# Index scores over all 128 contraction rows, and half of layer 0's modulation moved beside them

## The chip, the cores and the metric

The kernel runs on one core of a Trainium2 chip. The metric is the device time of one execution in microseconds (us). Five engines work side by side, each with its own instruction stream: TensorE (PE; its weight loads are listed as PEld), VectorE (DVE), ScalarE (ACT), GpSimd (POOL) and SyncE (SP, whose queue issues the DMAs). They wait for one another by semaphores. The profile was taken of one execution on the chip; L12 is line 12 of the kernel.

## The reference, cut to what matters

The program is a two-layer encoder trunk over 1024 positions of width 1024. Each sub-layer is modulated by a vector that comes from a conditioning row c:

```python
cond = jax.nn.silu(c)
mod = (cond @ ada_w[l] + ada_b[l])[:, None, :]
sh_m, sc_m, g_m, sh_f, sc_f, g_f = jnp.split(mod, 6, axis=-1)     # parts 0 to 5
h = x * (1.0 + sc_m) + sh_m
y = even_mixer(h, ...)                                            # layer 0
x = layer_norm(DN_ALPHA * x + (1.0 + g_m) * y, ...)
h = x * (1.0 + sc_f) + sh_f
y = conv_ffn(h, ...)
x = layer_norm(DN_ALPHA * x + (1.0 + g_f) * y, ...)
```

Layer 0's mixer is a sparse attention beside a short gated convolution. One projection `z = h @ w_in` gives q, k, v, the index queries `q_idx` (8 heads of 64), one index key `k_idx` of 64, the weights of the index heads and the three inputs of the convolution. For each block of 128 queries an index score picks the 256 keys that the attention may see:

```python
rel = relu(einsum('bthd,bsd->bths', q_idx, k_idx))
score = einsum('bths,bth->bts', rel, w_idx)
_, idx = lax.top_k(where(admissible, score, NEG), 256)
```

Parts 0 and 1 of the modulation are needed before the projection. Parts 2 to 5 of layer 0 are needed later: part 2 when the mixer's output projection is added to the residual, parts 3 and 4 in the norm behind it, part 5 in the feed-forward net.

## The kernel before, in words

**Precision.** A float32 product is made of three matmuls of a 32-bit format with fewer mantissa bits (fp32r): each operand is split into a high part (ACT casts it) and a low part (DVE or POOL subtracts), and high times high, high times low and low times high are summed in PSUM. `mm3` (L288 to L290) is this triple; a projection of 512 positions is 8 of them, thus 24 matmuls over 128 rows and 512 columns.

**Index queries and keys.** The index head has only 64 dimensions, so the kernel stacks: for each head, `stack` (to L1299) puts the high part of the query into 64 rows of the tile `qi[:, head]` and the low part into the other 64. Even heads have the high part in rows 0 to 63, odd heads in rows 64 to 127. The key's high part `kih` and low part `kil` stand twice each, in both halves of the rows.

**Scores.** `index` (L1528) goes over query blocks i from 7 down to 2, and inside over four heads; it is called twice, for heads 0 to 3 and 4 to 7. For each head `scores2` makes a score tile of 128 queries by (i+1)*128 keys in a PSUM tile `idx_s` (two buffers), in pieces of 512 keys or fewer. Each piece is a pair of matmuls: L1307 takes all 128 rows of `qi` with `kih` (high and low query times high key), L1308 only the 64 rows with the high part with `kil`. ACT applies relu into `rl` (two buffers, L1537); DVE adds it, times the head's weight, to the block's score `dd[i]` (L1540, L1542). Behind each head `index` takes 1.4 (first call) or 1.6 (second call) steps from a generator of projections, each one `mm3`; these are what PE does between scores.

**Search.** The 256th largest score of each row is found by a bit search over 31 bits. Per bit, DVE proposes a candidate (L1618), ACT counts by signs in three blocks (L1624), DVE counts in the other three (L1576), then DVE decides (L1636, L1637). In this stage the order of DVE and ACT is the written one. Each bit also takes `mods.step()`, and nine of ten advance the projections by one product of 512 positions. When a product is finished, its result is copied out and, for each second one, the next weight is split (L266 on ACT, L267 on DVE). Behind the bits come an exact step, the counts and the masks (L1642 to L1672), and then the attention.

**Modulation.** `Modulation` holds a list of (part, block) pairs. A step loads a 128x1024 block of `ada_w` (512 KB) and multiplies it by the row silu(c), summing along the row, in one DVE instruction (L377). Behind the eighth block of a part the bias is added (L340, L342). Before the change the 32 steps of parts 2 to 5 are all in the search; their blocks go into the buffers `eq` and `pre` in turn, and silu(c) stands in a PSUM tile `cond_row`.

**What sets the order.** PE runs in the order in which the program is written. In the index stage the order of the other engines comes from a planner; its costs and priorities are not touched here. SP issues the DMAs of one queue in order.

Of the kernel before, what the change touches and what calls it, by code (L numbers as in the profile page):

```python
# [20 lines left out]
D = 1024  # L21
# [185 lines left out]
def trunk(ctx, tc, t, out):  # L207
    nc = tc.nc
    V, A, G, T = nc.vector, nc.scalar, nc.gpsimd, nc.tensor

    def pool(name, bufs=1, side="left", space=None):
        if space is not None:
            return tc.tile_pool(name=name, bufs=bufs, space=space, reuse_waits="tile")
        return tc.tile_pool(name=name, bufs=bufs, side=side, reuse_waits="tile")
# [12 lines left out]
    def spend(us):  # L227
        clock[0] += us
# [21 lines left out]
    def bank(name):  # L250
        return mm.tile([P, HALF], F32, tag="mm", name=name)
# [3 lines left out]
    def bank2(name):  # L255
        return aux[0].tile([P, S], F32, tag="s", name=name)
# [4 lines left out]
    def half(hf):  # L261
        return slice(hf * HALF, (hf + 1) * HALF)

    def split(hi, lo, src, lo_eng="dve"):

        A.copy(hi, src)  # L266
        (V if lo_eng == "dve" else G).tensor_tensor(lo, src, hi.bitcast(F32), ALU.subtract)  # L267
# [1030 lines left out]
            A.copy(dst[n][own, c], src[own])  # L1298
            V.tensor_tensor(dst[n][rest, c], src[own], dst[n][own, c].bitcast(F32), ALU.subtract)  # L1299

    def scores2(ps, i, q, kh, kl, rows):

        qc = slice(i * P, (i + 1) * P)
        w = (i + 1) * P
        for c in range(0, w, HALF):
            e = min(c + HALF, w)
            T.matmul(ps[:, c:e], lhsT=q[:, qc], rhs=kh[:, c:e], start=True, stop=False)  # L1307
            T.matmul(ps[:, c:e], lhsT=q[rows, qc], rhs=kl[rows, c:e], start=False, stop=True)  # L1308
            spend(2 * max(e - c, 256) / 2400.0)


# [16 lines left out]
    start = ExitStack()  # L1328
    tmp0 = start.enter_context(pool("start", bufs=3))
    bias0 = bias_of(0, tmp0)  # L1330
    kih = ip.tile([P, S], F32R, name="kih")
    kil = ip.tile([P, S], F32R, name="kil")
    wiT = ip.tile([P, S], F32, name="wiT")
    wi = ip.tile([P, 8, 8], F32, name="wi")
    qi = ip.tile([P, 8, S], F32R, name="qi")
# [67 lines left out]
    for hf in range(2):  # L1403
        c = half(hf)
        ps = first[0][2][:, c]
# [10 lines left out]
    def more_queries(m, w=None):  # L1416

        halves = range(2) if w is None else range(1, 2)
        w = w or weights(t["w_ev"][m], f"qi{m}")
        for hf in halves:  # L1420
            ps = bank("qi")
            for k, x in enumerate(h.xs(hf)):
                o = slice(k * P, (k + 1) * P)
                mm3(ps, (w[0][:, o], w[1][:, o]), x, k == 0, k == KD - 1)
                if k == KD - 1:
                    stack((qi[:, 2 * m], qi[:, 2 * m + 1]), ps, half(hf))
                yield
# [4 lines left out]
    ps = bank("wit")  # L1432
# [11 lines left out]
    class Projections:  # L1444
# [75 lines left out]
        def taps(self, m):  # L1520
            u, y = self.conv["u"], yb[:, m]
            A.mul(y, u[:, 0:S], ctap[:, m, 0:1])
            for k in (1, 2):
                V.scalar_tensor_tensor(
                    y, u[:, k : k + S], ctap[:, m, k : k + 1], y, ALU.mult, ALU.add
                )

    def index(heads, others, rate):  # L1528
        n = 0.0
        for i in range(7, 1, -1):  # L1530
            w_ = (i + 1) * P
            for hd in heads:
                rows = slice(64 * (hd % 2), 64 * (hd % 2) + 64)
                ps = bank2("idx_s")
                scores2(ps, i, qi[:, hd], kih, kil, rows)
                rl = tmp.tile([P, S], F32, tag="rl", name="rl")
                A.activation(rl[:, :w_], ps[:, :w_], AF.Relu)  # L1537
                wc = wi[:, i, hd : hd + 1]
                if hd == 0:
                    V.tensor_scalar(dd[i], rl[:, :w_], wc, None, ALU.mult)  # L1540
                else:
                    V.scalar_tensor_tensor(dd[i], rl[:, :w_], wc, dd[i], ALU.mult, ALU.add)  # L1542
                n += rate
                while n >= 1.0:
                    next(others, None)
                    n -= 1.0
    products = Projections().steps()
    index(range(4), chain(more_queries(3), products), FILL[0])
    index(range(4, 8), products, FILL[1])
    ipx.close()  # L1550
    yb = evy.enter_context(pool("evyb")).tile([P, 4, S], F32, name="yb")
    evkv = ExitStack()
# [14 lines left out]
    tk = sel.enter_context(pool("tk", side="right"))  # L1567
    eq = tk.tile([P, S], F32, name="eq")
    pre = tk.tile([P, S], F32, name="pre")
    junk = [tk.tile([P, S], BF16, name=f"junk{e}") for e in "va"]  # L1570

    cond_row = bank2("cond_row")
    mods = Modulation(None, tk, 0, range(2, 6), D, 0, cond_row, (eq, pre))

    def count(cnt, d, w, thr, op):
        V.tensor_scalar(junk[0][:, :w], d, thr, 0.0, op, ALU.add, accum_out=cnt)  # L1576
# [99 lines left out]
    def advance():  # L1676
        while next(products, True) is False:
            pass
# [3 lines left out]
    with tc.manual_schedule(engines={E.DVE}):  # L1682
        rows_ = Rows()
        rows_.setup()
        with tc.manual_schedule(engines={E.Activation}):
            pace = 0.0
            for bit in range(30, -1, -1):
                rows_.propose(bit)
                rows_.signs()
                rows_.counts()  # L1690
                mods.step()
                pace += PACE
                if pace >= 1.0:
                    advance()
                    pace -= 1.0
                rows_.decide()
            advance()
            mods.step()
        for nm, src in (("q", q32), ("k", k32)):
            split(*pairs[0, nm], src[:, 0])  # L1700
        rows_.step_up()
        rows_.result()
        rows_.mask()
# [147 lines left out]
    with ExitStack() as s:  # L1851
# [35 lines left out]
        for hf in range(2):  # L1887
            c = half(hf)
            xs = h.xs(hf)
            for base, n, mi, lo in ((4, 3, 0, 0), (7, 2, 1, 3)):  # L1890
# [18 lines left out]
                for m in range(n):  # L1909
                    ps = blocks[m][0]  # L1910
# [14 lines left out]
            for m in (3, 0, 1, 2) if hf else range(4):  # L1925
                w = weights(t["w_od"][m], f"u{hf}_{m}", lo_eng="pool")
                ps = bank("u")
# [33 lines left out]
    with ExitStack() as s:  # L1961
# [97 lines left out]
        for j in range(8):  # L2059
            ps = bank("uv")  # L2060
# [63 lines left out]
def build(nc, arrays):  # L2124
    t = {
        k: nc.dram_tensor(f"in_{k}", v.shape, mybir.dt.from_np(v.dtype), kind="ExternalInput").ap()
        for k, v in arrays.items()
    }
    out = nc.dram_tensor("out_xT", (KD, P, S), F32, kind="ExternalOutput").ap()
    with tile.TileContext(nc, schedule_with_timeline_sim=True) as tc:  # L2130
        trunk(tc, t, out)
# [15 lines left out]
```

## Time and profile before

| | us |
|---|---|
| median of the 3 runs shown (lowest, highest) | 2689.89 (2680.07, 2691.18) |
| the profiled execution | 2674.74 |
| its span, first to last instruction | 2672.9 |

| engine | busy us | share of the span |
|---|---|---|
| PE | 2467.4 | 92% |
| PEld | 1936.7 | 72% |
| DVE | 2157.8 | 81% |
| ACT | 1364.8 | 51% |
| POOL | 1054.5 | 39% |

The table is read as an average over stages with different limits. Matmuls are pipelined and their ends are modelled: in the timeline one bar reaches into the next, and the distance from start to start is what a matmul costs. The mean granted clock of TensorE is 0.969 of full speed; the low level is 0.50 in this unit.

### The profile page before, as it was taken

What the parts mean: (1) busy time and instruction counts of PE and PEld (TensorE: products, weight loads), DVE (VectorE), ACT (ScalarE), POOL (GpSimd) and SP (SyncE); (2) the same over time, 40 slices, a digit from 0 to 9 for tenths busy, and PEclk for the clock granted to TensorE, in tenths of its full rate; (3) what the DMA queues carried; (4) which work ended last, traced back from release to release, by engine and by line L of the source; (5) the groups of instructions that cost most, each with busy time, mean ns of one, the idle gap of its engine ahead of it and who ended that gap; (6) DMA issues with size and microseconds to landing.
All of it is one profiled execution on the core that took longest, in us unless ns stands there. A gap on an engine that the chain in (4) does not pass through costs nothing. (4 is left out here: it accounts for less than half of the span.)

```text
span 2672.9 us, 32638 instructions
## 1 busy us (share of the span) xinstructions
PE 2467.4 (92%) x10922; PEld 1936.7 (72%) x10922; DVE 2157.8 (81%) x3491; ACT 1364.8 (51%) x2427; POOL 1054.5 (39%) x800
## 2 busy tenths in 40 slices
PE   6999998999888989998999899999888999998997
PEld 5567776887666767786777677787666888877786
DVE  6549899777698999978887866877698877788977
ACT  3446751765554444554333546766464555563434
POOL 0000001645674222424547634643865333334546
PEclk9899999999989989999999999999989999999999
DMA  6004430013434555335323331123533322244313
GB/s 244 32 18 136 139 118 16 17 68 120 129 104 153 183 173 166 126 98 178 91 75 95 105 101 61 54 75 106 173 100 103 107 86 84 95 128 148 102 47 105
DMA packets 123690, 284.43 MB, mean 106 GB/s; under 512 B 15361, under 2 KB 23042, under 8 KB 122626
## 3 DMA queue, kind: packets, MB, share of 16 engines
q1 hardware_dynamic: 122370, 278.16, 32.8%
q10 hardware_dynamic: 1152, 4.19, 0.4%
q8 instruction: 86, 1.41, 0.2%
q14 instruction: 82, 0.67, 0.1%
HBM read 234.06 MB, written 48.23 MB: 106 GB/s over the span
## 5 line engine op out<-in xcount | busy, mean ns | idle before, releaser
L702 DVE SCALAR_TENSOR_TENSOR cv<-u,taps,cv 128x512 f32<-128x512 f32 x352 | 311.1, 910 | 19.1 <-ACT cv L700 17.5
L267 POOL TENSOR_TENSOR v<-v,v 128x512 fp32r<-128x512 f32 x8 | 12.6, 1580 | 443.6 <-ACT v L266 443.6
L998 DVE SCALAR_TENSOR_TENSOR r<-dn,mod,r 128x512 f32<-128x512 f32 x198 | 147.0, 745 | 44.4 <-PE dn L290 42.5
L833 POOL TENSOR_TENSOR s<-rawg 128x512 f32<-128x512 f32 (+3 forms) x60 | 79.4, 1323 | 256.4 <-DVE wlo_ups L267 87.3
L700 ACT ACTIVATE cv<-u,taps 128x512 f32<-128x512 f32 x176 | 124.3, 721 | 58.0 <-DMA z<-cv 32.8
L288 PE MATMUL up<-t,wh 128*128 128x512 f32 x288 | 119.5, 415 | 33.1 <-ACT u L872 33.1
L706 ACT ACTIVATE cv<-cv 128x512 f32<-128x512 f32 x88 | 55.6, 632 | 144.7 <-DVE cv L702 143.9
L289 PE MATMUL up<-h_f,whi_up 128*128 128x512 f32 x256 | 105.5, 412 | 24.8 <-DVE h_f L267 24.8
L872 ACT COPY u<-up 128x512 f32<-128x512 f32 x144 | 83.9, 583 | 75.8 <-issue 35.3
L267 DVE TENSOR_TENSOR wl<-rawg,wh 128x512 fp32r<-128x512 f32 (+3 forms) x120 | 116.1, 970 | 2.6 <-ACT wh L266 2.4
L289 PE MATMUL up<-t,wh 128*128 128x512 f32 x288 | 117.7, 409 | 0.0
L290 PE MATMUL up<-t,wl 128*128 128x512 f32 x288 | 117.3, 407 | 0.0
L288 PE MATMUL up<-h_f,whi_upa 128*128 128x512 f32 x288 | 114.6, 398 | 1.2 <-ACT whi_upa L266 1.2
L834 POOL TENSOR_TENSOR s<-s,raw_upv 128x512 f32<-128x512 f32 x36 | 51.4, 1428 | 161.9 <-DMA raw_upv<-in_w_up 145.7
L266 ACT CAST wh<-rawg 128x512 fp32r<-128x512 f32 (+3 forms) x120 | 65.0, 545 | 97.6 <-PE dn L289 52.4
L290 PE MATMUL up<-h_f,wlo_upa 128*128 128x512 f32 x288 | 113.7, 395 | 0.7 <-DVE wlo_upa L267 0.7
L267 DVE TENSOR_TENSOR pl<-pt,ph 128x128 fp32r<-128x128 f32 (+2 forms) x192 | 99.4, 546 | 18.3 <-ACT ph L266 18.1
L266 ACT CAST ph<-pt 128x128 fp32r<-128x128 f32 (+2 forms) x192 | 85.3, 480 | 54.6 <-PE pt L1197 53.1
L289 PE MATMUL up<-h_f,whi_upa 128*128 128x512 f32 x288 | 113.0, 392 | 0.0
L290 PE MATMUL up<-h_f,wlo_up 128*128 128x512 f32 x256 | 104.6, 409 | 6.0 <-POOL wlo_up L267 6.0
L288 PE MATMUL up<-h_f,whi_up 128*128 128x512 f32 x256 | 106.4, 416 | 2.9 <-ACT h_f L266 1.9
L1624 ACT ACTIVATE junka<-dd,cand 128x384 bf16<-128x384 f32 (+2 forms) x93 | 87.1, 936 | 39.9 <-DVE cand L1618 37.9
(750 smaller groups left out, 8617.3 us busy)
## 6 DMA issues: line engine op xcount, KB each, us to landing
mod_raw<-in_ada_w SPq DMA_DIRECT2D x96, 256.0 KB, 2.9
z<-cv SPq DMA_DIRECT2D x88, 256.0 KB, 2.0
raw_upv<-in_w_up SPq DMA_DIRECT2D x36, 512.0 KB, 3.7
rawg<-in_w_up SPq DMA_DIRECT2D x34, 512.0 KB, 3.7
raw_up<-in_w_up SPq DMA_DIRECT2D x32, 512.0 KB, 3.7
z<-z SPq DMA_DIRECT2D x56, 256.0 KB, 2.9
xa_dram<-xo SPq DMA_DIRECT2D x48, 256.0 KB, 2.1
raw_dr<-in_w_dr SPq DMA_DIRECT2D x32, 384.0 KB, 3.1
```

Source lines behind the costliest of these rows:

```text
L266: A.copy(hi, src)
L267: (V if lo_eng == "dve" else G).tensor_tensor(lo, src, hi.bitcast(F32), ALU.subtract)
L288: T.matmul(ps, lhsT=wh, rhs=xh, start=start, stop=False, skip_group_check=more)
L289: T.matmul(ps, lhsT=wh, rhs=xl, start=False, stop=False, skip_group_check=more)
L290: T.matmul(ps, lhsT=wl, rhs=xh, start=False, stop=stop, skip_group_check=more)
L700: A.activation(y[n], u[:, 0:HALF], AF.Copy, scale=self.taps[:, c, 0:1])
L702: V.scalar_tensor_tensor(y[n], u[:, k : k + HALF], self.taps[:, c, k : k + 1], y[n], ALU.mult, ALU.add,)
L706: A.activation(y[1], y[1], AF.Silu)
L833: G.tensor_tensor(s1, g[:, c0], g[:, c1], ALU.add)
L872: A.copy(dst, ps)
L998: V.scalar_tensor_tensor(r, ps, self.gate[:, dt : dt + 1], r, ALU.mult, ALU.add)
L1624: A.activation(junk[1][:, :w], d, AF.Sign, bias=self.col(self.cand.bitcast(F32), j), scale=-1.0, accum_out=self.col(self.cnt, j),)
```

## The change

Three edits. `scores2` no longer takes the 64 rows of its second matmul: L1308's instruction covers all 128 rows of `qi` and `kil`, so that low query times low key is summed too. A modulation object for parts 2 and 3 is made before the index scores, with a pool of its own (three load buffers of 512 KB in all partitions, a row of c, a bias), and steps once behind each even head of the blocks 7 to 3, up to its 16 steps: ten in the first call of `index`, six in the second. The search keeps parts 4 and 5: 16 steps, at odd bits and once behind the loop.

```diff
-    def scores2(ps, i, q, kh, kl, rows):
+    def scores2(ps, i, q, kh, kl):
...
             T.matmul(ps[:, c:e], lhsT=q[:, qc], rhs=kh[:, c:e], start=True, stop=False)
-            T.matmul(ps[:, c:e], lhsT=q[rows, qc], rhs=kl[rows, c:e], start=False, stop=True)
+            T.matmul(ps[:, c:e], lhsT=q[:, qc], rhs=kl[:, c:e], start=False, stop=True)
...
+    modx = ExitStack()
+    modp = modx.enter_context(pool("modp"))
+    mods = Modulation(modp, modp, 0, range(2, 4), D, 3)
+
     def index(heads, others, rate):
...
             for hd in heads:
-                rows = slice(64 * (hd % 2), 64 * (hd % 2) + 64)
                 ps = bank2("idx_s")
-                scores2(ps, i, qi[:, hd], kih, kil, rows)
+                scores2(ps, i, qi[:, hd], kih, kil)
+                if i > 2 and hd % 2 == 0:
+                    mods.step()
...
     index(range(4, 8), products, FILL[1])
+    modx.close()
     ipx.close()
...
-    mods = Modulation(None, tk, 0, range(2, 6), D, 0, cond_row, (eq, pre))
+    mods = Modulation(None, tk, 0, range(4, 6), D, 0, cond_row, (eq, pre))
...
                 rows_.counts()
-                mods.step()
+                if bit % 2:
+                    mods.step()
```

## Rows read from the trace of the kernel before

**Rows 1.** The page, part 1: busy us, share of the span, instructions of each engine.
```profile
PE 2467.4 (92%) x10922; PEld 1936.7 (72%) x10922; DVE 2157.8 (81%) x3491; ACT 1364.8 (51%) x2427; POOL 1054.5 (39%) x800
```

**Rows 2.** Windows, index stage: us; busy (instructions) PE, PEld, DVE, ACT, POOL; PEclk, DMA, GB/s.
```profile
82.60:96.40 13.80, 13.80 (x26) 7.23 (x26) 3.74 (x5) 3.07 (x3) 0.00 (x0) 0.50 0.00 0
96.40:199.00 102.60, 102.60 (x345) 60.84 (x345) 45.71 (x51) 41.91 (x58) 0.00 (x0) 1.00 0.05 16
```

**Rows 3.** Waits from 83 to 199 us: total us, times, longest.
```profile
ACT rl L1537 <- PE idx_s L1308: 69.6, 46, 3.6
```

**Rows 4.** Timeline of PE, one score pair between projections: start, duration, instruction.
```profile
128.63 0.39 PE L1307 MATMUL idx_s<-kih,qi 128*128 128x512 f32 x1
128.95 0.49 PE L1308 MATMUL idx_s<-kil,qi 64*128 64x512 f32 x1
129.37 0.50 PE L288 MATMUL q<-h_m,whi_q 128*128 128x512 f32 x1
129.70 0.40 PE L289 MATMUL q<-h_m,whi_q 128*128 128x512 f32 x1
129.94 0.39 PE L290 MATMUL q<-h_m,wlo_q 128*128 128x512 f32 x1
```

**Rows 5.** Timeline of PE, first attention scores behind the last projection.
```profile
448.50 0.39 PE L290 MATMUL bg<-h_m,wlo_('bg', 3)_2958 128*128 128x512 f32 x1
448.82 0.44 PE L288 MATMUL s<-kh,qh 64*128 64x384 f32 x1
449.10 0.34 PE L289 MATMUL s<-kl,qh 64*128 64x384 f32 x1
449.28 0.34 PE L290 MATMUL s<-kh,ql 64*128 64x384 f32 x1
```

**Rows 6.** Windows of the search and of the wait before the attention.
```profile
211.00:376.00 165.00, 156.75 (x672) 124.92 (x671) 149.12 (x360) 121.04 (x224) 0.00 (x0) 0.98 0.45 134
...
450.00:460.00 10.00, 0.83 (x5) 0.47 (x3) 9.86 (x11) 0.00 (x0) 0.00 (x0) 0.74 0.00 0
```

**Rows 7.** Timeline of DVE in the search: two bits (of 31), from proposal to proposal.
```profile
231.81 0.17 DVE L1618 TENSOR_TENSOR cand<-small,bits 128x6 int32<-128x6 int32 x1
...
236.20 0.17 DVE L1618 TENSOR_TENSOR cand<-small,bits 128x6 int32<-128x6 int32 x1
...
239.06 1.22 DVE L377 CUSTOM_DVE_ANT_0 eq<-eq,cond_row 128x1024 f32<-128x1024 f32 x1
240.20 0.08 DVE L377 DVE_READ_ACCUMULATOR2_ANT mod_acc<- 128x1 f32 x1
240.59 1.23 DVE L267 TENSOR_TENSOR wlo_('k', 3)_1590<-raw_('k', 3)_1513,whi_('k', 3)_1589 128x1024 fp32r<-128x1024 f32 x1 [0.32 <-ACT whi_('k', 3)_1589 L266]
...
242.14 0.17 DVE L1618 TENSOR_TENSOR cand<-small,bits 128x6 int32<-128x6 int32 x1
```

**Rows 8.** The tile idx_s: count, ns min/median/max, first and last start, forms.
```profile
L1308 PE MATMUL idx_s<-kil,qi x80: 323/491/793, 83.4 to 198.3; 64*128 64x512 f32 x48, 64*128 64x384 f32 x16, 64*128 64x256 f32 x8, 64*128 64x128 f32 x8
```

**Rows 9.** Timeline of PE in the stretch at the low clock.
```profile
89.00 0.79 PE L1308 MATMUL idx_s<-kil,qi 64*128 64x512 f32 x1
89.72 0.79 PE L288 MATMUL qi<-h_m,whi_qi 128*128 128x512 f32 x1
90.32 0.63 PE L289 MATMUL qi<-h_m,whi_qi 128*128 128x512 f32 x1
```

**Rows 10.** Timeline of ACT in the second of those bits.
```profile
239.43 0.19 ACT L1624 ACTIVATION_READ_ACCUMULATOR junka<-dd,cand 128x1 f32 x1
239.52 1.04 ACT L266 CAST whi_('k', 3)_1589<-raw_('k', 3)_1513 128x1024 fp32r<-128x1024 f32 x1
```

**Rows 11.** DMA issues: count, KB each, median us from issue to landing.
```profile
pre<-in_ada_w SPq DMA_DIRECT2D x16, 512.0 KB, 3.7
```

**Rows 12.** Timeline of PE and PEld among projections.
```profile
429.37 0.39 PE L289 MATMUL xb<-h_m,whi_('xb', 3)_2898 128*128 128x512 f32 x1
429.37 0.19 PEld L290 LDWEIGHTS xb<-h_m,wlo_('xb', 3)_2899 128*128 128x128 f32 x1
```

## The prediction

> **What bounds the kernel now.** I read the page first: TensorE (PE) is busy for 92% of the span, ahead of every other engine [rows 1]. That share is an average, so I looked up the two stages that the change touches by their windows. The index scores run from 82.6 to 199 us. PE is busy for all of these 116 us, first at the lower clock level (granted 0.50, 13.8 us), then at the full one; VectorE (DVE) is busy for 3.7 + 45.7 = 49.5 us and ScalarE (ACT) for 45 us, and DMA is nearly idle [rows 2]. The waits of that stretch say the same: ACT's relu waited 69.6 us for the score matmuls, in 46 waits [rows 3]. So the index stage is bound by PE.
>
> Next is what PE does in it. In the timeline a busy bar overlaps the next one, so the distance between starts is what counts. Full-height matmuls of 512 columns follow each other in 0.233 us (129.70 to 129.94 is one such step, rounded). Around a score pair it is slower [rows 4]: from the 128-row matmul to the 64-row one 0.32, from that to the next 0.42, and the projection behind the pair still takes 0.33. Each change between a 128-row and a 64-row matmul costs something on both of its sides. The attention shows that the change does it, and not the smaller height: there the first 64-row matmul starts 0.32 behind the 128-row one before it, the next (384 columns) 0.28 on, and from then on 64-row matmuls follow in 0.18 [rows 5].
>
> The search (31 bits, 211 to 376 us and the last one) is another case: PE is busy 156.8 of 165 us and DVE 149.1 [rows 6]. DVE's timeline gives 4.39 us for a bit with the modulation's multiply-and-sum, and 5.94 us for the next, in which a projection weight is split too [rows 7]; the two kinds alternate over most of the 31 bits. Behind the search DVE finishes the masks alone: from 450 to 460 us it is busy 9.9 us and PE 0.8 [rows 6].
>
> **The change, part by part.**
>
> Score matmuls. No instruction is added: the second matmul of each pair has the same columns and reads 128 rows where it read 64. What goes is the change of height. The three steps of the pair in [rows 4] take 0.32 + 0.42 + 0.33 = 1.07 us; dense they would take 3 x 0.233 = 0.70. That is 0.37 a pair, and there are 80 pairs [rows 8]. (Pairs with a narrower second piece differ by a few hundredths either way.) In the 13.8 us at the lower level PE gets through 26 matmuls [rows 2], 6 pairs among them. A pair costs more there: 0.72 from the 64-row matmul to the next and 0.60 behind that [rows 9], and 0.72 taken for the step inside the pair too, against 0.47 each (twice 0.233): 0.63. I assume that the low stretch keeps its length; then its 6 x 0.63 = 3.8 us are filled with work that would take half of that at the full level: 1.9. The other 74 pairs save 74 x 0.37 = 27.4. Sum 29.3 us; 27.4 if the low stretch gave nothing, 31.2 if it shrank with its work. The stage would last some 87 us. Were the cause another one, the least is 0; that is rival (c).
>
> Modulation beside the scores. Sixteen steps (parts 2 and 3) come in: each one load of 512 KB and one multiply-and-sum of 128x1024 on DVE, 1.22 us long, of which 1.14 pass before the next instruction (239.06 to 240.20) [rows 7]: 18.2 us. To that come a row of c (512 KB) and its Silu on ACT (about 1 us, taken from the cast of the same width in [rows 10]), one bias load, and one or two short additions per part. DVE would carry 49.5 + 19 = 68 us in a stage of 87, so PE hides it. The cover is thinnest in the first half, which takes ten of the sixteen: there a widest unit needs about 1.9 us of PE (four score matmuls 0.93, and 1.4 projection steps of 0.70), and DVE about 2.1 by an estimate from [rows 2, 7] (sum over heads 1.2, half a step 0.57, its share of weight and query splits 0.3). Two score buffers and two relu buffers stand between them, and the low stretch at the start leaves DVE idle. I take 1 us lost, with 0 and 18 (no cover at all) as ends. What queues behind such a step on DVE is the sum over heads; ACT's relu waits for that, then the score buffer, then PE. The loads pass SP's queue in between the projection weights; such a load lands in 3.7 us [rows 11], three buffers are filled ahead, and a step is due about each 3.8 us (two units). DMA has the room: 0.05 of it is used [rows 2], and 16 loads in 60 us are some 140 GB/s, near what the search moves (134 GB/s, a share of 0.45) [rows 6].
>
> Search with half its steps. Sixteen multiply-and-sums fall out, 18 us of DVE, but the search can't give them all back. The steps leave every second bit. In the first ten bits these are the 4.39 us ones. Without the 1.14 DVE would need 3.25, and then ACT decides: its last sign count ends 3.42 us behind the bit's proposal (236.20 to 239.62) [rows 7, 10], and deciding and proposing add some 0.5. So about 0.45 goes per bit. In the middle the order shifts by one, and the steps leave bits that split a weight. There the split waits for ACT's cast, which begins when the sign counts end and runs to 240.56, while the multiply ends at 240.28 [rows 7, 10]: nothing is gained in five bits. In the last third three of the bits hold another DVE instruction and may give 1.0. Together 7 x 0.45 + 3 x 1.0 + 1.1 for the last = 7.3 us at most. And PE, dense for 156.8 of the 165 us, has the same projections to do in between; its 8 us of gaps stand where ACT or DVE was late with a weight or a copy, and most of those stay. I take 4, ends 0 and 8. The masks behind the search are DVE's own work, so what the search saves starts the attention earlier; the 9 us for which PE waits there absorb a lag of PE.
>
> Sum against the profiled execution (span 2672.9 us, 2674.7 with what lies around it): -29.3 + 1 - 4 = -32.3, so 2642.4. The median of the runs shown is 2689.9, 15.2 above the profiled one, and the same step from there gives 2657.6; I say 2657.
>
> A page of the Trainium skill speaks against the first part. TensorE: Matmul & The Clock Gate, section The mechanism, says that a weight load overlaps running matmuls only when their row groups differ; in the changed kernel all are alike. The trace shows otherwise: the weight load at 429.37, 0.19 us long, runs beside a full-height matmul [rows 12], and these follow each other in 0.233 all the same, where 0.233 + 0.19 would be 0.42.
>
> **The rivals.**
> (a) The search gives more. If DVE's work alone set it, its 18 us would come back until PE's gaps are used up: 8 in the search and about half of the 9 behind it, some 14 instead of 4: -29.3 + 1 - 14 = -42, 2647. For it speaks DVE's 149 of 165 us; against it PE's 157, and that ACT stands right behind DVE.
> (b) DVE takes the index stage over. Each moved step costs its 1.14 on the path: -29.3 + 18 - 4 = -15, 2675. For it: in the first half DVE and PE are within 10% of each other. Against: the second half has six steps, and the low stretch is free.
> (c) The gaps don't come from the height (but, say, from two matmuls with one stationary tile in a row), so the first part doesn't do what it says: only the search gains, 2686. Against it stands [rows 5], where other tiles show the same loss at the change.
> (d) Slower: the loads come late. SP's queue is in order; if a modulation load stands behind a weight load that waits for its buffer, DVE waits for the landing in every step. At 3.7 us of wait, 16 x 4.84 = 77, DVE needs 127 us for the stage, 11 over today's 116: 11 - 4 = +7, 2697. It begins to cost from a wait of about 1.2 us a step ((87 - 49.5) / 16 - 1.14), and from 3.3 the kernel is slower. Against it: three buffers, and a DMA that is idle.
> (e) Weight loads no longer overlap: 0.42 for each of a pair's three steps, 1.26 where 1.07 stand now, +15 over 80 pairs, less 4: 2701. Against it: the projections. This is what the page named above would have.
>
> **How the numbers follow.** The forecast, with 26 to 32 us from the index stage and 0 to 8 from the search, gets 0.64, (a) 0.13, (b) 0.11, (c) 0.04, (d) 0.05, (e) 0.03. What a measurement of this kernel can tell from no change is about 0.5%, 13.4 us. Faster by more: the forecast, (a) and most of (b), 0.87. Within: (c) and the rest of (b), 0.07. Slower: most of (d) and (e), 0.06. The range runs from 2636 ((a), with 31.2 in the index stage and nothing lost there, and a median 8 lower as the runs spread) to 2676, just past (b).
>
> **What would show it.** In the new timeline each score matmul of 512 columns starts 0.23 behind the one before, also inside a pair and behind it. The index stage lasts 84 to 90 us with PE still dense and ACT's relu still waiting for PE. DVE shows sixteen 1.22 us steps there with next to no wait for DMA. In the search, bits without a step take about 4 us and those that split a weight still 5.9; the whole is shorter by less than 8. I am wrong in the first step if 0.32 and 0.42 stay inside and behind the pair, in the second if PE waits for the relu's buffer, in the third if the search falls by more than 10 us or not at all.

## The result, and the profile after

The changed kernel took 2652.7 us (median of 4 runs, 2647.2 to 2657.9) against 2687.9 for the kernel before (4 runs, 2680.1 to 2691.2): a ratio of 0.987, 95% interval 0.984 to 0.990, thus 26 to 42 us saved. The forecast was 2657, in a range of 2636 to 2676. Between the medians lie 35.2 us, where the forecast took off 32.3; it started from 2689.9, the median without the fourth run of the kernel before (2685.8). The profiled executions differ by 27.5 us (2674.74 and 2647.2).

The total came out as forecast, but its parts did not. From the timelines of both kernels I took five marks: the first and the last score matmul, the first proposal of the search, the copy that follows its last bit, and the first maximum of the attention.

| us | before | after | difference | forecast |
|---|---|---|---|---|
| index scores, first to last matmul | 115.7 | 90.1 | -25.5 | -28.3 |
| from there to the first proposal | 12.9 | 12.8 | -0.1 | 0 |
| search, 31 bits | 181.6 | 171.7 | -9.9 | -4 |
| exact step and masks | 66.6 | 73.1 | +6.5 | 0 |
| attention starts at | 459.4 | 431.3 | -28.1 | |
| from there to the end of the span | 2213.5 | 2214.1 | +0.6 | 0 |

(The index stage also begins 1.0 us later. Over all runs of this study that start lay between 82.4 and 84.4 us, so I read nothing into it.)

The page and the windows of the same stages, with the columns of [rows 1, 2, 6]. First the page of the changed kernel.

```profile
PE 2437.7 (92%) x10922; PEld 1939.6 (73%) x10922; DVE 2157.2 (82%) x3491; ACT 1365.3 (52%) x2428; POOL 1058.7 (40%) x800
```

Its windows: the index stage in three stretches, the search, and the end of the masks.

```profile
83.60:88.50 4.90, 4.90 (x13) 3.81 (x14) 4.84 (x9) 1.02 (x1) 0.00 (x0) 0.50 0.71 193
88.50:120.00 31.50, 26.33 (x111) 19.87 (x109) 29.84 (x46) 14.49 (x19) 0.00 (x0) 0.95 0.64 205
120.00:173.80 53.80, 53.80 (x247) 44.67 (x248) 32.06 (x37) 28.88 (x41) 0.00 (x0) 1.00 0.07 20
...
186.50:341.60 155.10, 149.05 (x646) 119.40 (x645) 132.21 (x328) 120.95 (x224) 0.00 (x0) 0.99 0.30 92
...
420.00:430.00 10.00, 0.00 (x0) 0.00 (x0) 9.82 (x9) 0.00 (x0) 0.00 (x0) 0.65 0.00 0
```

In the second stretch DVE is busy for 29.8 of 31.5 us and PE for 26.3 only: there, and only there, the index stage is no longer PE's. Its waits (83 to 168 us; before, [rows 3]) say on what:

```profile
ACT rl L1543 <- PE idx_s L1308: 25.2, 29, 2.7
...
ACT rl L1543 <- DVE dd L1548: 13.8, 8, 3.4
PEld idx_s L1307 <- ACT rl L1543: 8.2, 7, 3.0
PE idx_s L1307 <- ACT rl L1543: 5.0, 4, 2.5
...
DVE mod_raw L377 <- DMA mod_raw<-in_ada_w: 1.3, 2, 1.2
```

DVE's sum is late, so relu finds no buffer, so PE finds no score buffer: 5.0 us. Behind the longest of these waits (2.5 us) the granted clock fell to the low level once more:

```profile
109.00:112.40 3.40, 3.40 (x11) 2.54 (x10) 3.40 (x5) 1.06 (x2) 0.00 (x0) 0.50 0.69 247
```

That this second fall lengthens the stage is not shown: two kernels below that keep all sixteen steps in the planner's order and have no such fall need as long (91.1 and 89.9 us). The modulation's loads cost 1.3 us of DVE. DVE's timeline shows how its work got so tight: two steps in a row between two sums.

```profile
94.93 1.22 DVE L377 CUSTOM_DVE_ANT_0 mod_raw<-mod_raw,cond_row 128x1024 f32<-128x1024 f32 x1
...
96.07 1.22 DVE L377 CUSTOM_DVE_ANT_0 mod_raw<-mod_raw,cond_row 128x1024 f32<-128x1024 f32 x1
...
97.22 1.28 DVE L1548 SCALAR_TENSOR_TENSOR dd<-rl,wi,dd 128x1024 f32<-128x1024 f32 x1
```

All sixteen steps ran between 82.0 and 114 us. The program writes them behind every second unit up to the sixteenth, which in the written order (below) comes at 147 us; the planner, which orders DVE here, put them all into the first third of the stage.

PE's timeline answers to [rows 4]: the matmuls of a unit, and the projection behind it.

```profile
89.21 0.39 PE L1307 MATMUL idx_s<-kih,qi 128*128 128x512 f32 x1
89.44 0.40 PE L1308 MATMUL idx_s<-kil,qi 128*128 128x512 f32 x1
89.67 0.39 PE L1307 MATMUL idx_s<-kih,qi 128*128 128x512 f32 x1
89.90 0.39 PE L1308 MATMUL idx_s<-kil,qi 128*128 128x512 f32 x1
90.12 0.40 PE L288 MATMUL qi<-h_m,whi_qi 128*128 128x512 f32 x1
```

Each start is 0.22 to 0.23 behind the one before. The 0.32 and 0.42 are gone.

In the search (DVE, as [rows 7]) a bit without a step takes 3.80 us, one that splits a weight 5.93:

```profile
206.02 0.17 DVE L1625 TENSOR_TENSOR cand<-small,bits 128x6 int32<-128x6 int32 x1
...
209.82 0.17 DVE L1625 TENSOR_TENSOR cand<-small,bits 128x6 int32<-128x6 int32 x1
...
215.75 0.17 DVE L1625 TENSOR_TENSOR cand<-small,bits 128x6 int32<-128x6 int32 x1
```

And in the exact step and the masks DVE now waits. After (358.2 to 431.3 us):

```profile
ACT whi_('cg', 3)_2862 L266 <- PE cg L289: 4.8, 1, 4.8
DVE wlo_('cg', 3)_2863 L267 <- ACT whi_('cg', 3)_2862 L266: 3.8, 1, 3.8
...
DVE cx L1506 <- PE xb L290: 2.4, 3, 1.2
...
DVE wlo_('bg', 3)_2983 L267 <- ACT whi_('bg', 3)_2982 L266: 0.2, 1, 0.2
```

The first line leads DVE's longest wait, for ACT's cast of a weight, on to PE's projection. Before, in the same stage (392.8 to 459.4 us), ACT's cast waited for PE just as long, but all that DVE waited for was:

```profile
DVE cx L1506 <- PE xb L290: 0.3, 1, 0.3
```

3.8 + 2.4 + 0.2 - 0.3 = 6.1 of the 6.5 us by which that stage grew.

### The profile page after: what moved, and what is told of

Its sections match the earlier page's. It is cut to its first block, busy times and chain, and to the rows that moved or that the text cites. A ratio compares the mean times of both kernels' runs of the same rounds, so it can differ in the third digit from the quotient of the medians.

```text
span 2645.4 us, 32650 instructions
## 1 busy us (share of the span) xinstructions
PE 2437.7 (92%) x10922; PEld 1939.6 (73%) x10922; DVE 2157.2 (82%) x3491; ACT 1365.3 (52%) x2428; POOL 1058.7 (40%) x800
## 5 line engine op out<-in xcount | busy, mean ns | idle before, releaser
L700 ACT ACTIVATE cv<-u,taps 128x512 f32<-128x512 f32 x176 | 124.4, 721 | 53.1 <-DMA z<-cv 28.1
L288 PE MATMUL up<-t,wh 128*128 128x512 f32 x288 | 119.5, 415 | 29.3 <-ACT u L872 29.3
L377 DVE CUSTOM_DVE_ANT_0 mod_raw<-mod_raw,cond_row 128x512 f32<-128x512 f32 (+1 forms) x112 | 105.1, 944 | 17.7 <-DMA mod_raw<-in_ada_w 13.9
L289 PE MATMUL up<-h_f,whi_upa 128*128 128x512 f32 x288 | 113.0, 392 | 0.0
```

What stands on the lines that cost most here:

```text
L288: T.matmul(ps, lhsT=wh, rhs=xh, start=start, stop=False, skip_group_check=more)
L289: T.matmul(ps, lhsT=wh, rhs=xl, start=False, stop=False, skip_group_check=more)
L377: V.tensor_tensor_reduce(out=raw, in0=raw, in1=self.cond[:, o], scale=1.0, scalar=0.0, op0=ALU.mult, op1=ALU.add, accum_out=self.acc[:, j, ...
L700: A.activation(y[n], u[:, 0:HALF], AF.Copy, scale=self.taps[:, c, 0:1])
```

## The experiments

My theory, from these two profiles: the 128-row matmul gives more than the whole gain, and the moved modulation brings nothing, since it costs PE time in the index stage and what the search wins comes back as waits for PE's projections. The rival: the two edits add up, 25 us from the scores and 10 from the search. Within one profile the stage times are the sharper measure: from the attention to the end, where nothing was edited, the profiles of this study took 2213 to 2229 us.

| kernel | index | search | masks | attention at | ratio to before (95%) |
|---|---|---|---|---|---|
| before | 115.7 | 181.6 | 66.6 | 459.4 | |
| change | 90.1 | 171.7 | 73.1 | 431.3 | 0.987 (0.984 to 0.990) |
| rows alone | 81.2 | 179.2 | 66.3 | 423.4 | 0.985 (0.982 to 0.988) |
| modulation alone | 116.3 | 171.4 | 73.4 | 457.3 | 0.999 (0.997 to 1.001) |
| heights grouped | 99.8 | 180.8 | 66.2 | 442.4 | 0.993 (0.990 to 0.996) |
| steps spread | 91.1 | 171.7 | 73.1 | 432.5 | 0.989 (0.986 to 0.992) |
| written order | 84.4 | 171.8 | 71.6 | 423.6 | 0.987 (0.985 to 0.990) |
| two terms | 89.9 | 168.4 | 67.3 | 422.7 | 0.985 (0.983 to 0.988) |
| rows, fewer steps | 74.9 | 182.9 | 71.9 | 424.8 | 0.989 (0.986 to 0.992) |
| written order, pace 1.0 | 84.0 | 188.1 | 63.2 | 431.1 | 0.990 (0.987 to 0.992) |
| change again | 90.1 | 171.7 | 73.1 | 430.8 | 0.988 (0.985 to 0.990) |
| rows alone again | 81.2 | 180.4 | 66.5 | 423.3 | 0.987 (0.985 to 0.989) |
| written order, pace 0.8 | 83.4 | 168.3 | 74.1 | 422.9 | 0.987 (0.985 to 0.990) |
| rows, pace 0.8 | 81.9 | 173.2 | 75.5 | 425.7 | 0.987 (0.985 to 0.990) |

**Rows alone.**

```diff
-            T.matmul(ps[:, c:e], lhsT=q[rows, qc], rhs=kl[rows, c:e], start=False, stop=True)
+            T.matmul(ps[:, c:e], lhsT=q[:, qc], rhs=kl[:, c:e], start=False, stop=True)
```

> Only the first edit: the second score matmul takes 128 rows, all 32 modulation steps stay in the search. Theory (the change of height costs TensorE, and the moved modulation hardly pays): the index stage falls from 116 to some 85 us with no wait for the relu's buffer, less than the 90 of the full change; the search stays at 181 us and the masks at 67, so the whole comes out about 31 us below the kernel before, thus as fast as the full change or up to 4 us faster. Rival (the two edits add up, the search's half being worth the 10 us that the search lost): this kernel gains 18 to 25 us only and is 5 to 10 us slower than the full change.

Measured: the index stage 81.2 us, 34.5 below before and 8.9 below the full change. Its windows:

```profile
84.00:87.60 3.60, 3.60 (x10) 2.85 (x10) 0.79 (x3) 1.02 (x1) 0.00 (x0) 0.50 0.00 0
87.60:165.20 77.60, 77.60 (x359) 64.46 (x358) 48.21 (x54) 43.55 (x59) 0.00 (x0) 1.00 0.07 21
```

PE is dense throughout, and the stretch at the low clock lasts 3.6 us where it lasted 13.8 [rows 2]. The waits of that stage show none of PE for the relu's buffer. The rival falls: this edit by itself is not slower than both together (0.985 and 0.987), and its attention starts 7.9 us earlier.

**Modulation alone.** The change with the 64-row matmul put back.

```diff
...
-            T.matmul(ps[:, c:e], lhsT=q[:, qc], rhs=kl[:, c:e], start=False, stop=True)
+            T.matmul(ps[:, c:e], lhsT=q[rows, qc], rhs=kl[rows, c:e], start=False, stop=True)
...
```

> Only the second edit: sixteen modulation steps beside the index scores, the second score matmul keeps its 64 rows. Theory: the index stage, bound by TensorE at 116 us, hides the steps and stays within 1 us; the search falls by about 10 us, the masks behind it grow by about 6, so the whole gains 3 to 5 us. Rival (the edits add up as above): 8 to 10 us faster.

Measured: 0.999, interval -0.3% to +0.1%. The search gives 10.2 us, the masks take back 6.8, and the attention starts 2.1 us earlier; in the time nothing can be seen of that. While the scores are slow they do hide the steps (116.3). The interval ends at 8.6 us saved, so it leaves out most of the rival's 8 to 10 us but not all; the masks, which take back two thirds of what the search gives, speak against the rest.

**Heights grouped.** The kernel before, with the matmuls of a unit reordered.

```diff
             T.matmul(ps[:, c:e], lhsT=q[:, qc], rhs=kh[:, c:e], start=True, stop=False)
+        for c in range(0, w, HALF):
+            e = min(c + HALF, w)
             T.matmul(ps[:, c:e], lhsT=q[rows, qc], rhs=kl[rows, c:e], start=False, stop=True)
```

> The kernel before with one reordering: in each score unit all 128-row matmuls come first and then all 64-row ones. The 32 units of two pieces (blocks 7 to 4, 8 heads) have 2 changes of height each where they had 4. Theory (each change costs about 0.19 us): 32 x 2 x 0.19 = 12 us less in the index stage, some 104 us. Rival (the loss comes from two matmuls in a row with the same stationary tile): pairs of the same tile still follow each other, now two of equal height, so the stage stays at 116 us.

Measured: 99.8 us, 15.9 less. PE's timeline, one unit of two 512-column pieces and the projection behind it:

```profile
98.71 0.57 PE L1307 MATMUL idx_s<-kih,qi 128*128 128x512 f32 x2
99.21 0.67 PE L1310 MATMUL idx_s<-kil,qi 64*128 64x512 f32 x2
99.81 0.50 PE L288 MATMUL qi<-h_m,whi_qi 128*128 128x512 f32 x1
100.16 0.39 PE L289 MATMUL qi<-h_m,whi_qi 128*128 128x512 f32 x1
```

From 98.71 to 100.16 are 1.45 us for five steps; by [rows 4] the order of before needs 0.32 + 0.42 + 0.32 + 0.42 + 0.33 = 1.81, and dense it is 1.17. So 0.36 goes in each of 32 units, 11.5 us, near the 12 expected; beside that the low stretch was shorter, ending at 89.0 us here and at 96.4 before, which I take for the rest of the 15.9. The 64-row matmuls are as many as before and the gain is that of the changes taken away, so it is the changes of height that cost the time, and not the 64 rows as such. A stationary tile used twice in a row costs nothing either: in the changed kernel both matmuls of a pair have the same one and follow in 0.23. The Trainium skill has the rule in TensorEngine Tiling (Array Packing), section Key Properties: changing the tiling mode drains TensorE. The trace agrees in that each change costs time; that it is a drain it doesn't show. The price in this kernel is 0.37 us for a lone 64-row matmul between 128-row ones, and 0.28 for two in a row (1.45 less 1.17). The Trainium skill's other rule, in TensorE: Matmul & The Clock Gate, section The mechanism, that weight loads overlap running matmuls only where the row groups differ, is contradicted by the changed kernel as well: all its score matmuls have the same rows and a weight load each, 0.19 us long, and follow in 0.23.

**Steps spread.** The change with six steps in the first call of `index` and ten in the second.

```diff
-                if i > 2 and hd % 2 == 0:
+                if hd == 0 or (hd > 3 and hd % 2 == 0 and i > 2):
```

> The changed kernel with its sixteen steps spread otherwise: 6 in the first half of the index scores, 10 in the second (10 and 6 in the change). Theory (in the first half VectorE is the later one, and TensorE waits 5 us for the relu's buffer): that wait falls below 2 us and the index stage from 90 to 86 or 87; the whole is 3 to 4 us faster than the change. Rival (the wait comes from the loads or from the start): it stays at 5 us and so does the time.

Measured: no gain, 91.1 us, and PE's wait for the relu's buffer was 7.9 us where it had been 5.0. My edit didn't test whether the first half holds too much work, since the steps didn't move. The steps' instruction in this kernel:

```profile
L377 DVE CUSTOM_DVE_ANT_0 mod_raw<-mod_raw,cond_row x16: 1215/1220/1227, 82.2 to 114.2; 128x1024 f32<-128x1024 f32 x16
```

First and last start are 82.2 and 114.2, against 82.0 and 113.0 in the change: where the program writes them hardly mattered, the planner pulled them forward. The next kernel takes the planner out.

**Written order.** The change, but in the index stage DVE runs in the order in which the program is written, and no longer in the planner's.

```diff
...
-    index(range(4), chain(more_queries(3), products), FILL[0])
-    index(range(4, 8), products, FILL[1])
+    next(products)
+    w3 = weights(t["w_ev"][3], "qi3")
+    with tc.manual_schedule(engines={mybir.EngineType.DVE}):
+        index(range(4), chain(more_queries(3, w3, range(2)), products), FILL[0])
+        index(range(4, 8), products, FILL[1])
```

> The changed kernel, but in the index scores VectorE runs in the written order, so that the sixteen modulation steps come one behind every second unit; the planner had put all of them into the first 31 us of the stage, two or three between the sums. (The first two weight splits are made ahead of the stage, as they are in the change.) Theory (the planner's order, not the amount of work, makes TensorE wait 5 us for the relu's buffer): the wait goes, the index stage falls from 90 to 83 us at most, and the attention starts 6 to 8 us earlier, 2645 us. Rival (VectorE hasn't the room even when the steps are spread, as the estimate of 2.1 against 1.9 us a unit says): TensorE still waits 3 us or more and the stage stays above 86 us.

Measured: 84.4 us. The steps now run from 82.3 to 146.9 us, and PE's wait for relu's buffer falls from 5.0 to 1.0:

```profile
PE idx_s L1307 <- ACT rl L1543: 1.0, 2, 0.6
```

So the planner's order cost 5.7 of the 8.9 us by which the change's index stage is longer than that of the rows alone; 3.2 stay. Not all of these are the steps': the low stretch lasted 5.9 us here and 3.6 in the rows alone. With the same index stage and a low stretch of 3.7 us (the written order with pace 0.8) it took 83.4, so about 1 us goes with the clock and some 2 with the steps. The attention starts 7.7 us earlier than in the change. In the time (0.987 both) that could not be told apart.

**Two terms.** From k on, the projections leave out the product with the input's low part.

```diff
-                        mm3(ps, (w[n][0][:, o], w[n][1][:, o]), x, k == 0, k == KD - 1)
+                        if n < 4:
+                            mm3(ps, (w[n][0][:, o], w[n][1][:, o]), x, k == 0, k == KD - 1)
+                        else:
+                            T.matmul(ps, lhsT=w[n][0][:, o], rhs=x[0], start=k == 0, stop=False)
+                            T.matmul(ps, lhsT=w[n][1][:, o], rhs=x[0], start=False, stop=k == KD - 1)
...
```

> The changed kernel with a third of TensorE's work left out from the search on: the projections behind the queries (k, v and the convolution's) are made of two of the three terms, the low part of the input is left out; VectorE's and ScalarE's work stays. Theory (what the shorter search gains comes back as waits for TensorE's projections in the mask stage, 73 us where it had been 66): the mask stage falls to 67 us or less and the search by some 5 us more, so the attention starts 10 to 14 us earlier. Rival (the longer mask stage comes from VectorE's order or ScalarE): it stays at 73 us.

Measured: the masks fall to 67.3 us and the search by 3.2; the attention starts 8.6 us earlier, under the 10 to 14 expected. The 6 us that the masks had gained came from PE being late: with a third of its work gone, they are gone. Of the 244.8 us of search and masks in the change about 9 went with that third of PE's work. With it gone PE is busy for 131 of the search's 168 us and DVE for 147, so what is left is mostly DVE's and ACT's chain; that part is argued, not tried.

**Pace and fill.** Three kernels move projections between the stages: rows alone with `FILL = (1.4, 1.2)`, and the written order with `PACE = 1.0` and 0.8; a fourth is rows alone with `PACE = 0.8`.

> The 128-row matmul alone (all modulation in the search), and 1.2 instead of 1.6 projection steps behind each unit of the second half of the index scores: some 10 steps of 0.7 us, 7 us of TensorE, move behind the index stage. Theory (behind the index stage VectorE sets the end and TensorE waits 9.5 us before the attention): the index stage ends 7 us earlier, 2 to 4 of these are given back as waits for projections, and the whole is 3 to 5 us faster than with the rows alone, some 2640 us. Rival (TensorE is the bound there too): no change within 1 us, or slower.

> The kernel with the written order in the index scores, and the search advances the projections by one product in each bit (PACE 1.0) where it was nine in ten bits, thus three more products within the search. Theory (TensorE lags, and the waits move between search and masks): the search grows by 2 to 4 us, the mask stage falls from 73 to some 64, and the attention starts 4 to 7 us earlier than without. Rival (the mask stage's waits don't depend on how many products are left): it stays at 73, and the whole is slower by the 2 to 4 us.

> The changed kernel with the written order in the index scores, and a search that advances the projections by 0.8 product in a bit instead of 0.9. With 1.0 the search grew by 16 us and the masks shrank by 8. Theory (the search waits for TensorE, and the optimum lies lower now that VectorE's bits are shorter): the search falls by 5 to 8 us, the masks grow by 4 to 6, the attention starts 1 to 3 us earlier. Rival (0.9 is the balance): it starts 1 to 4 us later.

> The 128-row matmul alone, all modulation in the search, with 0.8 product in a bit. Theory (its bits are still long enough for 0.9): the search falls by 3 us at most, the masks grow by 5 or more, and the attention starts 1 to 4 us later than with the rows alone. Rival (as above): 1 to 3 us earlier.

Measured: fewer steps in the index scores shorten that stage by 6.3 us, and search and masks together take it back with interest (254.8 for 245.5): the rival was right, PE's work is missed later. Pace 1.0 lengthens the search by 16 us and shortens the masks by 8: the attention starts 7.5 us later, theory wrong. What it missed is that PE then bounds the search:

```profile
179.81:367.88 188.07, 186.59 (x816) 150.15 (x815) 149.69 (x356) 132.09 (x239) 0.00 (x0) 1.00 0.29 89
```

Pace 0.8 with the written order starts the attention 0.7 us earlier, with the rows alone 2.4 later (against 423.3): directions as expected, too small for the totals to show. The parts missed: with the written order the search fell by 3.5 us (5 to 8 expected), and with the rows alone by 7.2 (3 at most). For the written order 0.9 is near the balance; for the rows alone only the lower side was tried.

**Both once more, on one chip.**

> The changed kernel once more, unaltered, to stand on one chip beside the rows alone. Expected as measured: 27 to 40 us below the kernel before.

> The 128-row matmul alone once more, on the same chip as the full change. Theory (the moved modulation costs 9 us in the index stage and gives 2 to 4 behind it): 5 to 8 us faster than the full change. Rival (they are equal, and the difference between the two runs was that of two chips): within 2 us.

Measured: the stages repeat to 1.2 us, and the rows alone start the attention 7.5 us earlier. The times are 2651.7 (4 runs) and 2649.0 (5 runs), ratios 0.988 and 0.987 with overlapping intervals. My 5 to 8 us are not confirmed in the total: in the profiled executions the head start holds to the output projection (593.5 against 600.8 us) and is gone at the first matmul into the tile `dn` (1250.9 and 1251.0), where between the first two profiles it was still 6.8 us (1243.3 and 1250.1). The stages between, where nothing was edited, differ by as much from run to run. No kernel here is shown to beat the change.

## Why the prediction was right

The first step, the change of height, was right in mechanism and made the gain. That the total came so near is in part luck: against the forecast the scores gave 5 us more, the moved modulation cost 8 more, the search gave 6 more, and the masks cost 6.5 that the sum had at nothing.

**Score matmuls: right, sized low.** The mechanism held as written: starts at 0.23, PE dense in the rows alone; the rival (c) fell with the grouped kernel, and (e) with the starts at 0.23. The step forecast 29.3 us. The rows alone gave 34.5. A pair was sized well: outside the low stretch the saving is 34.5 less 6.5, thus 28.0, or 0.378 for each of 74 pairs (0.37). What failed was "I assume that the low stretch keeps its length": it fell from 13.8 to 3.6 us. Those 26 matmuls took 13.8 us [rows 2]; ten of them at the low clock and sixteen dense take 3.6 + 3.7 = 7.3. That is the 6.5, where the sum had 1.9.

**Modulation beside the scores: wrong in size.** I took 1 us with ends of 0 and 18; it is 8.9 (90.1 against 81.2). The failed step is the cover: I had shared the steps out evenly, one for two units, as the program has them, and the planner issued them in a burst. 5.7 us are its order, the other 3.2 the work and some 1 us of low clock. PE's wait for the relu's buffer, which the prediction named as the sign of being wrong here, came: 5.0 us. Rival (b) had this direction; DVE did take over 31.5 us of the stage, by the planner's order more than by the work. The loads were no trouble: 1.3 us of waits in all, so (d) falls.

**Search: right by its bits, low in sum.** Bits without a step came to 3.80 to 3.86 us (3.9 to 4.0 forecast), bits that split a weight kept 5.93, and four of the five in the middle gave nothing. Seven times 0.55 and three times 1.15 are 7.3, as much as the "at most" of the sum, though the last bit, for which the sum had 1.1, gave nothing. The other 2.6 came from two bits in the middle, 6.80 and 8.12 us long before and 4.88 and 7.24 after, and they go with the clock. Before, PE had been idle for 2.6 us just ahead of them, and the granted clock was low behind that; after, it was idle for 1.3 us and the clock stayed up:

```profile
281.00:287.40 6.40, 5.91 (x14) 4.71 (x15) 5.92 (x14) 5.43 (x10) 0.00 (x0) 0.50 0.35 94
...
253.00:266.00 13.00, 12.02 (x55) 9.77 (x56) 11.10 (x32) 9.97 (x20) 0.00 (x0) 1.00 0.32 88
```

The rows alone, with every step still in the search, had PE idle for 1.2 us, the clock up, and 4.60 and 7.52 us; their repeat had 2.7 us, the clock low for 3.3, and 5.48 and 8.11. So this gain can come without a step taken out. None of the five profiles with half the steps at this pace and three terms had the clock low there, three of the four with all the steps had: whether the steps bring it about is open. The sum of 9.9 us stays just under the 10 that the prediction gave as a sign of being wrong.

**Masks: wrong.** "The masks behind the search are DVE's own work, so what the search saves starts the attention earlier" was the failed sentence. DVE's order in that stage contains weight splits and products that wait for PE's projections, and with the search 9.9 us shorter DVE waited 6.1 us more for them. The net of both, -3.5, lies beside the forecast's -4 by two errors that cancel, as 29.3 - 1 lies beside 34.5 - 8.9. That is luck, in both places.

## What to carry to other kernels

Read starts, not busy bars: here a matmul of half height between full ones cost 0.37 us on top of its own 0.23, and filling the idle rows, in this case with a useful small term, took that away. Where an engine's order comes from a planner, as DVE's did here, work that is ready early is not spread out by writing it spread out. And when a stage feeds off another engine's backlog, a saving in it is first paid to the backlog: look at the sum of both stages, and try the two halves of a change apart.

## What the hardware showed unexpectedly

Behind PE's pause at 78 us (4.1 to 5.3 us long) every kernel began its scores at the low clock. Counted from the first score matmul, that stretch was 13.8 us in the kernel before (26 matmuls) and 15.0 in the modulation alone (27), the two with a change of height at every score matmul. In the twelve other profiles it was 3.4 to 6.2 us: 6.2 with the heights grouped (13), 4.9 and 5.6 in the change (13 and 14), 3.6 in both profiles of the rows alone (10). Among these the order says little, since one and the same index stage (the written order, in three kernels) had 5.9, 5.2 and 3.7. The step from there to 13.8 is larger than this spread: where PE's matmuls followed each other without the seams, or with half of them in the wide units, the clock rose sooner. What in the seams decides it was not tried.
